# A new opening for an eight-core decoder kernel: order of the first loads, dummy matmuls, a shared first norm, and three conversions moved

## Chip, cores, metric

The kernel runs on all 8 cores of one Trainium2 chip, with the sequence split between the cores. The metric is the device time of the slowest core, in microseconds (us). Cores 0 to 3 are one die, 4 to 7 the other. In some executions one die or both run at a lower granted clock ("slow" state). Fast runs are compared with fast runs. A second measure is the **mean core span**: over all runs of a kernel, every die whose four cores all had a granted clock of 0.994 or more gives the mean of its four spans; the table gives the mean over such dies and its standard error. It is not the metric. The chips are called A to F, since kernels are only comparable on one chip: the same kernel before has a mean core span of 4998 us on some and 4994 us on others.

## The reference, cut

Two layers over x of shape (4, 8192, 1024), in float32:

```python
for l in range(DEPTH):
    x = x + 0.5 * swiglu(rms_norm(x, ffn1_norm[l]), ...)      # D_FF = 2816
    proj = rms_norm(x, mix_norm[l]) @ w_in[l]                   # q, k, v, u
    x = x + concat(rms_norm(window_attention), rms_norm(pooling)) @ w_out[l]
    x = x + cross_attention(rms_norm(x), rms_norm(mem), ...)
    x = x + 0.5 * swiglu(rms_norm(x, ffn2_norm[l]), ...)
return rms_norm(x, final_norm)
```

Only the first `rms_norm`, the first SwiGLU, and the loads of weights in the first 700 of 5000 us matter here.

## The kernel before

Each core works through nine tiles of up to 512 columns, twice (two layers). Matmuls are bf16, and weights arrive in 512 KB slots held in two rings: "F" (`sb_fr`, 6 slots, FFN weights) and "M" (`sb_mr`, 4 slots, all others). Weights lie in HBM as float32. A slot is either loaded and cast on the way by a DMA that GpSimd issues, or read as bf16 by a DMA that the sync engine (SP) issues. For the second kind a **conversion** must have run first: a DMA from HBM to HBM, issued by GpSimd, that waits for a certain matmul so that conversions spread over time. In the views below, `wf` and `wm` are the float32 weights of the two rings, `wfb` and `wmb` their bf16 copies, and `wab` is a bf16 tensor that the kernel itself has computed before and that SP loads into M slots. A load that casts on the way is called a cast load.

```python
def convert(kind, a, s):
    ...
    P._wait(P.E["pool"], [(id(pe.sem), pe.cnt - LAG)])
    P.dma("pool", rows(dst), rows(src), writes=(buf[a][s], cvb[i]), box=cvbox[i])
...
pre_conv = conv_list("wm", 0, 5, 9) + conv_list("wf", 1, 0, PRE)      # 34 conversions
...
elif v in (0, 1):
    ...
    run(sprinkle(fs, fill) if v else fs[:80] + sprinkle(fs[80:], pre_conv[:10]))   # fill = pre_conv[10:]
```

`fs` is the list of steps of a stage and `sprinkle` spreads conversions evenly over it. So 10 conversions stand in what is called the second stage here (v = 0), none in its first 80 steps, and 24 in the third (v = 1).

The opening:

```python
def x_chunks(ti, reads=()):                       # x of one tile, in four pieces of 512 KB
    for j in range(NPC):
        P.dma("act" if j % 2 else "sp", ...)      # two queues
        if ti == 0 and j == 0:
            P.dma("sp", vecs[:, :], vecs_d, writes=(constb,))

def first_norm(ti, dst, dstb):
    for c in range(NCH):                          # squares: odd chunks on VectorE, even on ScalarE
        ...
    ...                                           # 8 matmuls with ones sum over channels
    st.fin_act()                                  # Ln, Exp on ScalarE -> rst
    run(raw(h_steps(ti, 0, key, dst, dstb, 0, full=True)))   # 8 scales x * gain * rst on VectorE

# v == -1
P._wait(P.E["pool"], P._deps(xbs[0][:4], ())); advance("F", 0)    # slot 0 after half of tile 0's x
P._wait(P.E["pool"], P._deps(xbs[0], ()));     advance("F", 1)    # slot 1 after all of it
first_norm(0, hF, hFb)
x_chunks(1, (xbs[0][6], xbs[0][7]))
P._wait(P.E["pool"], P._deps(xbs[1], ()))                         # all of tile 1's x
advance("F", AHEAD["F"])                                          # slots 2 to 5
...
run(raw(g0[:5]))             # tile 0: gate and up of hidden chunks 0 and 1 (slots 0, 1)
first_norm(1, hM, hMb)
run(raw(g0[5:9] + g1[:9]))   # tile 0: chunk 2 (slot 2), then tile 1: chunks 0 to 2
```

The softmax here doesn't subtract the row's maximum and nothing guards it: scores larger than these inputs give would overflow.

## Time and profile before

| | us |
|---|---|
| median of 3 runs | 5008.35 (5007.73 to 5011.33) |
| core 0, the slowest in the profiled run | 5010.5 |
| the other seven cores | 4990.2 to 5000.8 |
| TensorE busy on core 0 | 4932.9 |

The first part of the profile's page gives busy time, share and number of instructions of each engine:

```profile
PE 4932.9 (98%) x25669; PEld 2437.3 (49%) x25669; DVE 2501.2 (50%) x4251; ACT 1666.9 (33%) x2862; POOL 983.1 (20%) x1058
```

TensorE is busy for 98%. Whatever the change wins must come out of the remaining 78 us, or out of matmuls that ran at half clock. The waits of TensorE on core 0 before 40 us (what ended the wait, us in total, how often, longest):

```profile
PE ps L351 <- DVE sb_kcarL L1198: 10.6, 1, 10.6
PE ps L351 <- DMA sb_fr<-wf: 3.5, 1, 3.5
PE ps L351 <- DVE sb_hF L488: 2.6, 1, 2.6
PE ps L351 <- DVE sb_pT L1209: 0.6, 1, 0.6
```

The first wait is for the matrix of ones, which VectorE fills only after the constants (`vecs`) have landed at 9.8 us, the third is Ln, Exp and the first scale, and the second is slot 2. The timeline of core 0 shows how these come about. Its columns are start, duration, engine, line, operation, output<-inputs, count, and in brackets the idle time before and what ended it:

```profile
8.60 1.15 ACT L149 ACTIVATE sb_pT<-sb_x 128x512 bf16<-128x512 f32 x2 [8.60 <-DMA sb_x<-xT]
9.81 0.43 DVE L1195 TENSOR_TENSOR sb_vecs<-sb_vecs 128x4 f32<-128x4 f32 x2 [9.81 <-DMA sb_vecs<-vecs]
12.25 1.15 ACT L149 ACTIVATE sb_pT<-sb_x 128x512 bf16<-128x512 f32 x2 [2.50 <-DMA sb_x<-xT]
16.66 5.39 DVE L488 SCALAR_TENSOR_TENSOR sb_hF<-sb_x,sb_vecs,sb_rst 128x512 bf16<-128x512 f32 x8 [3.10 <-ACT sb_esink L149]
17.56 12.48 PE L351 MATMUL ps<-sb_hF,sb_fr 128*128 128x512 bf16 x32 [2.63 <-DVE sb_hF L488]
...
28.14 2.11 POOL L159 DMA_DIRECT2D sb_fr<-wf  x4 [14.81 <-DMA sb_x<-xT]
35.21 3.61 PE L351 MATMUL ps<-sb_hF,sb_fr 128*128 128x512 bf16 x16 [3.46 <-DMA sb_fr<-wf]
38.66 10.52 PE L351 MATMUL ps<-sb_hM,sb_fr 128*128 128x512 bf16 x48
```

Half of tile 0's x is there at 8.6 us and the rest at 12.2. GpSimd waits until 28.1 us for tile 1's x before it asks for slot 2, and slot 2 ends TensorE's wait at 35.2 us. Tile 1's first gate matmul comes at 38.7. This last start is the marker for the opening below.

Much later, a second place that the change touches (timeline of core 0, same columns). A conversion goes out 0.57 us ahead of a cast load of an M slot, on the same queue, and TensorE then waits 4.6 us for that slot:

```profile
406.95 0.58 POOL L159 DMA_DIRECT2D wfb<-wf  x1
407.52 0.58 POOL L159 DMA_DIRECT2D sb_mr<-wm  x1
420.96 5.28 PE L351 MATMUL ps<-sb_hM,sb_mr 128*128 128x384 bf16 x16 [4.62 <-DMA sb_mr<-wm]
```

The 16 matmuls after the wait take 5.28 us; a warm group of 16 of this shape takes 2.76.

### The profile page before, as it was taken

The page shows a single profiled execution, that of the slowest core. Times are in us where ns is not written, and L with a number is a line of the kernel's source. Part 1 is how long each engine was busy: PE and PEld are TensorE (multiplying, and loading weights), DVE is VectorE, ACT ScalarE, POOL GpSimd, SP SyncE. Part 2 cuts the span into 40 slices and gives each one's busy share as a digit, 9 for nine tenths or more (in the row PEclk, how much of TensorE's full clock was granted, in tenths as well). Part 3 has the DMA queues.
Part 4 walks back from the last instruction along what each step waited for, and adds up shares of the span by engine and source line. Part 5 has one row for each costly group of instructions (what it writes and reads, how often), then busy time and mean ns, then how long its engine had stood idle before and what let it go on. Part 6 is the DMA issues. An engine that isn't in the chain of part 4 may idle for free.

```text
span 5010.5 us, 80089 instructions; the slowest of 8 cores (4990.2 to 5010.5 us)
## 1 busy us (share of the span) xinstructions
PE 4932.9 (98%) x25669; PEld 2437.3 (49%) x25669; DVE 2501.2 (50%) x4251; ACT 1666.9 (33%) x2862; POOL 983.1 (20%) x1058
## 2 busy tenths in 40 slices
PE   8999999999999999999999999999999999999998
PEld 3544454444454555554554544444444456455444
DVE  3245654454535363645454564635446454546452
ACT  3334432233332333332332333323323333333351
POOL 1222211212121121212120212211121212121111
PEclk9999999999999999999999999999999999999999
DMA  9998976677676887776786654444545556555434
GB/s 200 205 228 189 199 199 201 189 214 200 176 239 188 254 232 220 211 226 190 212 215 207 194 190 151 161 164 150 179 151 193 169 198 206 190 183 181 156 130 154
DMA packets 279558, 963.88 MB, mean 192 GB/s; under 512 B 30064, under 2 KB 31536, under 8 KB 278896
## 3 DMA queue, kind: packets, MB, share of 16 engines
q1 hardware_dynamic: 218016, 788.33, 48.3%
q0 software_dynamic: 60560, 168.32, 18.1%
q8 instruction: 221, 3.62, 0.3%
q10 hardware_dynamic: 576, 2.10, 0.1%
q14 instruction: 185, 1.52, 0.1%
HBM read 992.18 MB, written 130.02 MB: 224 GB/s over the span
## 4 chain that ended last, share of the span: by engine, by line
PE 91%; DMA 3%; DVE 2%; ACT 2%; issue 1%; POOL 0%; DVEq 0%; ACTq 0%; SPq 0%; POOLq 0%
PE ps L351 91%; DMA sb_fr<-wfb 1%; DMA sb_mr<-wm 1%; DMA sb_fr<-wf 1%; ACT sb_tmp L149 1%; ACT L146 1%; DVE sb_hM L488 0%; DVE sb_hF L488 0%; DMA sb_mr<-wab 0%; ACT sb_pT L149 0%; ACT sb_rst L149 0%; DVE sb_pT L843 0%; DVE sb_x L626 0%; DMA sb_x<-xT 0%; DVE sb_ao L891 0%
## 5 line engine op out<-in xcount | busy, mean ns | idle before, releaser
L351 PE MATMUL ps<-sb_hF,sb_fr 128*128 128x512 bf16 (+2 forms) x12320 | 2503.6, 360 | 25.0 <-DMA sb_fr<-wfb 8.8
L351 PEld LDWEIGHTS ps<-sb_hF,sb_fr 128*128 128x128 bf16 x12320 | 1201.7, 98 | 1234.5 <-issue 51.0
L351 PE MATMUL ps<-sb_act,sb_fr 128*128 128x512 bf16 (+2 forms) x6160 | 1263.2, 360 | 3.4 <-DMA sb_fr<-wf 2.7
L460 POOL TENSOR_TENSOR sb_acc<-sb_acc,sb_sqf 128x512 f32<-128x512 f32 (+3 forms) x522 | 627.9, 1203 | 2209.5 <-ACT sb_sqf L149 2142.7
L584 DVE TENSOR_TENSOR sb_act<-ps,sb_sg 128x512 bf16<-128x512 f32 (+2 forms) x770 | 489.7, 639 | 1061.4 <-PE ps L351 742.8
L351 PEld LDWEIGHTS ps<-sb_act,sb_fr 128*128 128x128 bf16 x6160 | 591.3, 98 | 616.3 <-issue 41.1
L149 ACT ACTIVATE sb_sg<-ps 128x512 f32<-128x512 f32 (+2 forms) x792 | 436.9, 557 | 1215.8 <-PE ps L351 941.5
L351 PE MATMUL ps<-sb_hM,sb_mr 128*128 128x512 bf16 (+2 forms) x3600 | 767.7, 359 | 6.3 <-DMA sb_mr<-wm 4.6
L149 ACT ACTIVATE sb_sqf<-sb_x 128x512 f32<-128x512 f32 (+2 forms) x553 | 324.0, 587 | 889.3 <-DVE sb_x L960 370.1
L351 PEld LDWEIGHTS ps<-sb_hM,sb_mr 128*128 128x128 bf16 x3600 | 352.0, 98 | 359.7 <-issue 13.9
L149 ACT ACTIVATE sb_pT<-ps 128x512 bf16<-128x512 f32 (+3 forms) x438 | 232.0, 561 | 375.0 <-PE ps L351 363.5
L626 DVE SCALAR_TENSOR_TENSOR sb_x<-ps,sb_x 128x512 f32<-128x512 f32 (+2 forms) x288 | 183.5, 637 | 259.3 <-PE ps L351 259.3
L720 DVE TENSOR_TENSOR sb_tmp<-ps,sb_sin 32x512 f32<-32x512 f32 (+2 forms) x360 | 229.1, 636 | 81.9 <-PE ps L351 52.1
L351 PE MATMUL ps<-sb_pT,sb_mr 128*128 128x512 bf16 (+4 forms) x1344 | 254.2, 345 | 9.6 <-DVE sb_pT L1120 3.7
L488 DVE SCALAR_TENSOR_TENSOR sb_hF<-sb_x,sb_vecs,sb_rst 128x512 bf16<-128x512 f32 (+2 forms) x280 | 218.0, 829 | 19.7 <-ACT sb_rst L149 16.6
L488 DVE SCALAR_TENSOR_TENSOR sb_hM<-sb_x,sb_vecs,sb_rst 128x512 bf16<-128x512 f32 (+2 forms) x296 | 191.5, 710 | 20.3 <-ACT sb_rst L149 20.3
L351 PEld LDWEIGHTS ps<-sb_pT,sb_mr 128*128 128x128 bf16 x1344 | 129.3, 98 | 130.1 <-issue 16.0
L960 DVE TENSOR_TENSOR sb_x<-ps,sb_x 128x512 f32<-128x512 f32 (+2 forms) x144 | 91.9, 639 | 185.1 <-PE ps L351 185.1
L1152 DVE TENSOR_TENSOR sb_x<-ps,sb_x 128x512 f32<-128x512 f32 (+2 forms) x144 | 92.1, 640 | 158.6 <-PE ps L351 158.6
L460 POOL TENSOR_TENSOR sb_ach<-sb_acc,sb_sqf 128x512 bf16<-128x512 f32 (+3 forms) x99 | 119.1, 1203 | 247.3 <-ACT sb_sqf L149 209.9
L149 ACT ACTIVATE sb_tmp<-sb_tmp 128x512 f32<-128x512 f32 (+3 forms) x204 | 124.5, 610 | 102.9 <-DVE sb_tmp L875 84.9
L146 ACT ACT_TABLE_LOAD x115 | 147.5, 1283 | 2.4 <-issue 0.3
(113 smaller groups left out, 2376.5 us busy)
## 6 DMA issues: line engine op xcount, KB each, us to landing
sb_fr<-wfb SPq DMA_DIRECT2D x1117, 512.0 KB, 4.7
sb_mr<-wmb SPq DMA_DIRECT2D x155, 512.0 KB, 4.6
sb_mr<-wab SPq DMA_DIRECT2D x144, 512.0 KB, 4.5
wfb<-wf POOLq DMA_DIRECT2D x96, 512.0 KB, 9.3
sb_fr<-wf POOLq DMA_DIRECT2D x38, 512.0 KB, 18.1
wfb<-sb_fr SPq DMA_DIRECT2D x36, 512.0 KB, 12.6
x<-sb_x POOLq DMA_DIRECT2D x20, 512.0 KB, 18.8
sb_x<-x POOLq DMA_DIRECT2D x20, 512.0 KB, 16.4
```

Of the source, the lines that this page charges most:

```text
L146: self.E["act"].h.preload_act_table_set(need)
L149: return self.op("act", lambda h: h.activation(out=out, in_=in_, func=func, scale=scale, **kw), reads, writes)
L351: P.op("pe", lambda h: h.matmul(out_ap, lt, rh, start=st, stop=sp_, skip_group_check=True), reads=list(rb), writes=(ob_,), signal=(i == n ...
L460: P.op("pool", lambda h: h.tensor_tensor(out=o[:, :T], in0=acc[a][:, :T], in1=sqf[s][:, :T], op=ALU.add), (accb[a], sqfb[s]), (ob_,))
L488: P.op("dve", lambda h: h.scalar_tensor_tensor(out=out_ap, in0=in_ap, scalar=vcol(col), in1=r[0], op0=ALU.mult, op1=ALU.mult), (in_b, r[1] ...
L584: P.op("dve", lambda h: h.tensor_tensor(out=a_, in0=d[1][0][:, :T], in1=sg[si][:, :T], op=ALU.mult), (d[1][1], sgb[si]), (ab_,))
L626: P.op("dve", lambda h: h.scalar_tensor_tensor(out=x_, in0=pp[:, :T], scalar=0.5, in1=x_, op0=ALU.mult, op1=ALU.add), (ppb, xb_), (xb_,))
L720: P.op("dve", lambda h: h.tensor_tensor(out=t1[lo:lo + 32, :W - c0], in0=pp[hi:hi + 32, :W - c0], in1=sinS[pr][lo:lo + 32, c0:W], op=ALU.m ...
L960: P.op("dve", lambda h: h.tensor_tensor(out=x_, in0=pp[:, :T], in1=x_, op=ALU.add), (ppb, xb_), (xb_,))
L1152: P.op("dve", lambda h: h.tensor_tensor(out=x_, in0=pp[:, :T], in1=x_, op=ALU.add), (ppb, xb_), (xb_,))
```

## The change

Intent: load tile 0's x in order on one queue, with the constants on the other; run 24 dummy matmuls meanwhile so that TensorE's clock is up; share the first norm's scales between VectorE and GpSimd; interleave gate and up of the first hidden chunk, so that both advance as scales come in; issue tile 1's x earlier, and let slots 2 to 5 wait for only half of it. Besides, 13 instead of 10 conversions go into the second stage.

```diff
 def x_chunks(ti, reads=()):
-        P.dma("act" if j % 2 else "sp", ...)
-        if ti == 0 and j == 0:
-            P.dma("sp", vecs[:, :], vecs_d, writes=(constb,))
+        P.dma("sp", ...)
...
+P.op("dve", lambda h: h.memset(actF[:, 0, :], 0.0), writes=(actb[0],))
 x_chunks(0)
-P.dma("sp", esink...); P.dma("sp", invc...)
+P.dma("act", vecs...); P.dma("act", esink...); P.dma("act", invc...)
+warm = ps_next()
+mms([(warm[0][:, :], warm[1], ones[:, :], actF[:, 0, :], (onesb, actb[0]), True, True) for _ in range(WARM)])   # 24
+ps_free(warm)
...
 def first_norm(ti, dst, dstb):
+    gc = (1, 4, 7)          # tile 0: x * gain of these chunks ahead of time on VectorE
...
     if ti == 0:
+        for c in (0, 2, 1, 3, 5, 4, 6, 7):
+            if c in gc: rstd_to(...)      # GpSimd: (x * gain) * rst
+            else:       scale_to(...)     # VectorE, as before
...
+                if pair and hc == 0:      # f_gu: gate and up of chunk 0 alternate, matmul by matmul
...
-first_norm(0, hF, hFb)
 x_chunks(1, (xbs[0][6], xbs[0][7]))
-P._wait(P.E["pool"], P._deps(xbs[1], ()))
+first_norm(0, hF, hFb)
+P._wait(P.E["pool"], P._deps(xbs[1][:4], ()))
...
-fill = pre_conv[10:]
+fill = pre_conv[13:]
-run(sprinkle(fs, fill) if v else fs[:80] + sprinkle(fs[80:], pre_conv[:10]))
+run(sprinkle(fs, fill) if v else fs[:80] + sprinkle(fs[80:], pre_conv[:13]))
```

More of the change, by code (lines that the diff above doesn't have):

```diff
@@ L40 @@
 NCV = 24
+WARM = 24
 PRE = 30
@@ L485, in done, with gain_to, rstd_to @@
                 give("rst", self.ri)
+        def gain_to(out_ap, out_b, in_ap, in_b, col):
+            P.op("dve", lambda h: h.tensor_scalar(out=out_ap, in0=in_ap, scalar1=vcol(col), scalar2=None, op0=ALU.mult), (in_b, constb), (out_b,))
+        def rstd_to(out_ap, out_b, in_ap, in_b, r):
+            P.op("pool", lambda h: h.tensor_tensor(out=out_ap, in0=in_ap, in1=r[0], op=ALU.mult), (in_b, r[1]), (out_b,))
         def scale_to(out_ap, out_b, in_ap, in_b, col, r):
@@ L558, in act_second, with f_gu @@
             return ubf[:, c:c + T], ub[g]
-        def f_gu(ti, l, f, src=None, act=act_main, shared=None):
+        def f_gu(ti, l, f, src=None, act=act_main, shared=None, pair=False):
             T = wide(ti, l) if f == 1 else tiles[ti][1]
@@ L587, in ev, with both @@
                     ps_free(d[1])
-                steps.append((lambda g=mmg: g(0), mmw(8, T)))
-                steps.append((lambda g=mmg: g(1), mmw(8, T)))
+                def both(hc=hc, d=d):
+                    slot, slb = d["slot"] = shared[hc] = load("F", "wf", l * 2 + f - 1, hc)
+                    d[0], d[1] = ps_next(), ps_next()
+                    mms([(d[part][0][:, :T], d[part][1], slot[:, (part * 8 + kc) * 128:(part * 8 + kc + 1) * 128], h_[:, kc, :T], (slb, hb_[kc]), kc == 0, kc == 7)
+                         for kc in range(8) for part in range(2)])
+                if pair and hc == 0:
+                    steps.append((both, mmw(16, T)))
+                    steps.append((lambda: None, 0.0))
+                else:
+                    steps.append((lambda g=mmg: g(0), mmw(8, T)))
+                    steps.append((lambda g=mmg: g(1), mmw(8, T)))
                 steps.append((ev, 0.0))
@@ L1185, in x_chunks @@
                 cs = slice(j * CPP, (j + 1) * CPP)
-                P.dma("act" if j % 2 else "sp", xw(ti, o + T)[:, cs, :], xblk(xT_d, OVER + c0 - o, o + T, j), reads=reads, writes=tuple(xbs[ti][cs]))
-                if ti == 0 and j == 0:
-                    P.dma("sp", vecs[:, :], vecs_d, writes=(constb,))
+                P.dma("sp", xw(ti, o + T)[:, cs, :], xblk(xT_d, OVER + c0 - o, o + T, j), reads=reads, writes=tuple(xbs[ti][cs]))
+        P.op("dve", lambda h: h.memset(ones[:, :], 1.0), writes=(onesb,))
+        P.op("dve", lambda h: h.memset(actF[:, 0, :], 0.0), writes=(actb[0],))
         x_chunks(0)
-        P.dma("sp", esink[:, :], sinkc_d, writes=(sinkb,))
-        P.dma("sp", invc[:, :], invc_d, writes=(invb,))
-        for l in range(L):
-            g0 = l * NVL + 44
-            P.op("dve", lambda h: h.tensor_tensor(out=vecs[:, g0:g0 + 4], in0=vecs[:, g0:g0 + 4], in1=vecs[:, g0 + 4:g0 + 8], op=ALU.mult), (constb,), (constb,))
-        P.op("dve", lambda h: h.memset(ones[:, :], 1.0), writes=(onesb,))
+        P.dma("act", vecs[:, :], vecs_d, writes=(constb,))
+        P.dma("act", esink[:, :], sinkc_d, writes=(sinkb,))
+        P.dma("act", invc[:, :], invc_d, writes=(invb,))
+        warm = ps_next()
+        mms([(warm[0][:, :], warm[1], ones[:, :], actF[:, 0, :], (onesb, actb[0]), True, True) for _ in range(WARM)])
+        ps_free(warm)
         for l in range(L):
@@ L1211, in first_norm @@
                     P.act(pT[:, c, :T], x_, AF.Square, (b_,), (pTb[c],))
+                if ti == 0 and c % 2:
+                    for g in gc:
+                        if g // 2 == c // 2:
+                            x_, b_ = xt(ti, 0, True)[g]
+                            gain_to(ao[:, gc.index(g), :T], aob[gc.index(g)][0], x_, b_, g)
             st.ps = ps_next()
@@ L1216, in first_norm @@
             if ti == 0:
-                P.act(esink[:, :], esink[:, :], AF.Exp, (sinkb,), (sinkb,))
-            run(raw(h_steps(ti, 0, key, dst, dstb, 0, full=True)))
+                for c in (0, 2, 1, 3, 5, 4, 6, 7):
+                    x_, b_ = xt(ti, 0, True)[c]
+                    if c in gc:
+                        rstd_to(dst[:, c, :T], dstb[c], ao[:, gc.index(c), :T], aob[gc.index(c)][0], st.r)
+                    else:
+                        scale_to(dst[:, c, :T], dstb[c], x_, b_, c, st.r)
+                st.done()
+                P.act(esink[:, :], esink[:, :], AF.Exp, (sinkb,), (sinkb,))
+                for l in range(L):
+                    g0 = l * NVL + 44
+                    P.op("dve", lambda h: h.tensor_tensor(out=vecs[:, g0:g0 + 4], in0=vecs[:, g0:g0 + 4], in1=vecs[:, g0 + 4:g0 + 8], op=ALU.mult), (constb,), (constb,))
+            else:
+                run(raw(h_steps(ti, 0, key, dst, dstb, 0, full=True)))
         def late_consts():
@@ L1322, in _build @@
                 advance("F", 1)
+                x_chunks(1, (xbs[0][6], xbs[0][7]))
                 first_norm(0, hF, hFb)
-                x_chunks(1, (xbs[0][6], xbs[0][7]))
-                P._wait(P.E["pool"], P._deps(xbs[1], ()))
+                P._wait(P.E["pool"], P._deps(xbs[1][:4], ()))
                 advance("F", AHEAD["F"])
@@ L1330, in _build @@
                 shared = {}
-                g0 = f_gu(0, 0, 1, shared=shared)
+                g0 = f_gu(0, 0, 1, shared=shared, pair=True)
                 g1 = f_gu(1, 0, 1, src=(hM, hMb), act=act_second, shared=shared)
```

## The prediction

> **Bound now.** The tensor engine: the page gives it 4932.9 of 5010.5 us busy (98%); the chain of waits is 91% matmul. Only part of core 0's 78 us of idle tensor time can be won, plus matmuls at half clock. By the tensor engine's waits, 17.3 us of it lies before 40 us: 10.6 us until the first ones-matmul, 2.6 us for Ln, Exp and first scale, 3.5 us for the third weight slot. Later ones the change can touch: 1.9 us at 106 us (wm slot), 4.6 us at 417 us (wm), 2.5 us (wab) and 1.8 us (wfb) at 630 to 690 us.
>
> **Opening before (timeline, core 0).** x's first half lands at 8.6 us, the rest at 12.2. VectorE waits for vecs to 9.8 us. First FFN matmul at 17.56; eight paced by 0.66 us scales, then half clock (0.43 us each) to about 27. Half of tile 1's x is issued by ScalarE at 16 us, behind Exp, and lands at 27.6; GpSimd then issues slots 2 to 5 at 28.1; DMA is empty from 26.3 to 29.7; slot 2 lands at 35.1, the dense stream starts at 35.2, tile 1's first gate matmul at 38.7.
>
> **The change.**
> 1. x in order on one queue, no vecs wait: the last piece lands at 11 to 12.5 us (slot 0's load starts earlier and competes), but one square per engine then remains: Exp about 1 us sooner.
> 2. GpSimd takes three scales (about 1.2 us each, from its other 128x512 operations), VectorE five: the first 16 matmuls end near 20 us, not 26.
> 3. 24 dummy matmuls, about 8 us in idle time. The Trainium skill ("TensorE: Matmul & The Clock Gate", Part 1) gives 3.4 us windows for warming and cooling; this trace roughly agrees (4.3 us of dense work before 0.43 became 0.22; after 3.2 us idle cores 1 and 3 were cold, core 0 after 3.5 us was not). Warmth may be lost again, and the next term binds anyway: about 0.
> 4. Tile 1's x all on the sync queue, not behind Exp: complete near 24 to 26 us. GpSimd waits for half of it: slots 2 to 4 issued near 20 us, slot 2 lands near 29 to 30. Main term. Tile 1's norm ends near 35 us, not 38.8. Together the dense stream shifts by 3.5 to 6 us; I take 4.5.
> 5. Three conversions move from the third stage (473 to 690 us) to the second (350 to 472). At 407 us a conversion went out 0.6 us ahead of the wm load on the same queue; with 13 spread evenly the nearest earlier one falls about 8 us sooner. The stall at 417 us (4.6 us on core 0, 0.9 to 2.8 on four others) and the half-clock matmuls after it (clock 0.72) mostly go: about -5 us on core 0, slowest by 10 us. Fewer later conversions: about -1.
> 6. Given back: DMA is saturated from 40 to 300 us, so slot waits near 106 and 200 us grow: +1.5.
>
> Sum: 5008.35 - 4.5 - 5 - 1 + 1.5 = about 4999.4 us, range 4991 to 5006. Faster by over 2%: 1%; within: 98%; slower: 1%.
>
> **Signs.** Right: slots 2 to 4 issued near 20 us; tile 1's first gate matmul near 33 to 35 us on core 0; no DMA gap at 26 to 30 us; the 417 us wait gone. Wrong: x landing after 13 us; a longer third-slot wait; new slot waits in 350 to 470 us.
>
> **What would make it wrong.** One queue moving x more slowly than two; GpSimd scales slowed beside VectorE; another core setting the time; conversions colliding with another load.

## The result

| | before | after |
|---|---|---|
| median, us | 5008.04 (4 runs, 5007.33 to 5011.33) | 5009.7 (4 runs, 5005.3 to 5013.83) |
| ratio of fast runs, 95% interval | | 1.0002 (0.9985 to 1.0019) |

The ratio is the mean time of one kernel's fast runs over that of the other's of the same rounds, so it is not quite the ratio of these medians. Nothing was gained: the forecast, 4999.4 of 5008.35 us, is a ratio of 0.9982 and lies just outside the interval.

The first line of the page (now of core 4, the slowest), then the core view of the profiled run after (span and granted clock), cut after core 5:

```profile
PE 4918.4 (98%) x25322; PEld 2440.5 (49%) x25693; DVE 2503.5 (50%) x4252; ACT 1666.3 (33%) x2862; POOL 987.9 (20%) x1061
```

```profile
core 0: 5001.1 us, clock 0.996
core 1: 4990.0 us, clock 0.997
core 2: 4989.4 us, clock 0.998
core 3: 4999.3 us, clock 0.997
core 4: 5012.3 us, clock 0.995
core 5: 5002.7 us, clock 0.996
```

The page's matmul counts cannot be set against each other, because some records are missing from the trace after. Core 0 went from 5010.5 to 5001.1 us, close to what was predicted for it, which was luck (see "The slowest core" below). Core 4 went from 5000.8 to 5012.3. Averaged over the eight cores of the two profiled runs the span is 4997.7 us before and 4998.9 after.

**The opening after.** TensorE's waits on core 0 before 40 us:

```profile
PE ps L352 <- DVE sb_hF L495: 4.3, 2, 3.7
PE ps L352 <- DMA sb_fr<-wf: 3.0, 2, 1.9
PE ps L352 <- ACT sb_pT L150: 2.4, 2, 1.4
PE ps L352 <- DVE sb_kcarL L1214: 2.0, 1, 2.0
```

The 10.6 us wait is gone from the list only because dummy matmuls fill it. The timeline of core 0 after:

```profile
13.18 0.63 ACT L150 ACTIVATE sb_pT<-sb_x 128x512 bf16<-128x512 f32 x1 [1.00 <-DMA sb_x<-xT]
16.64 6.52 DVE L495 SCALAR_TENSOR_TENSOR sb_hF<-sb_x,sb_vecs,sb_rst 128x512 bf16<-128x512 f32 x5 [2.35 <-ACT sb_esink L150]
16.68 4.60 POOL L492 TENSOR_TENSOR sb_hF<-sb_ao,sb_rst 128x512 bf16<-128x512 f32 x3 [2.28 <-ACT sb_esink L150]
18.64 2.72 PE L352 MATMUL ps<-sb_hF,sb_fr 128*128 128x512 bf16 x6 [3.67 <-DVE sb_hF L495]
24.43 2.18 POOL L160 DMA_DIRECT2D sb_fr<-wf  x4 [3.15 <-DMA sb_x<-xT]
26.50 3.61 PE L352 MATMUL ps<-sb_hF,sb_fr 128*128 128x512 bf16 x16 [1.11 <-DMA sb_fr<-wf]
33.70 3.61 PE L352 MATMUL ps<-sb_hF,sb_fr 128*128 128x512 bf16 x16 [1.87 <-DMA sb_fr<-wf]
37.15 1.67 PE L352 MATMUL ps<-sb_hM,sb_fr 128*128 128x512 bf16 x7
```

Slots 2 to 5 are asked for at 24.4 instead of 28.1 us. But on this core the last piece of x lands 0.9 us later (13.2), five scales on VectorE now take 6.52 us where eight took 5.39, and tile 1 starts at 37.2 us, 1.5 us sooner than before. Means over the eight cores, read from the same views:

| start, us | before | after |
|---|---|---|
| slot 0 asked for (half of tile 0's x landed) | 8.32 | 9.76 |
| slot 1 asked for (all of it landed) | 12.67 | 12.67 |
| first scale | 16.56 | 15.65 |
| first FFN matmul | 17.45 | 17.65 |
| slots 2 to 5 asked for | 28.00 | 23.60 |
| end of tile 1's last square on ScalarE | 28.18 | 27.94 |
| slot 2 first used | 34.45 | 32.96 |
| tile 1's first gate matmul | 38.91 | 37.73 |

So the opening gave 1.2 us at this marker in this pair of profiles. The eight cores of one profile differ there with a standard deviation of 2.3 us, so the size needs the repeats below.

**Where it went.** Each tile's mixer copies its last keys once, on GpSimd. These copies, "carry copies" in the expectations, cut the run into stages (timelines of core 0, before):

```profile
314.23 0.29 POOL L734 COPY sb_kcarL<-sb_kz 128x128 bf16<-128x128 bf16 x1 [17.81 <-DVE sb_kz L728]
492.05 0.29 POOL L734 COPY sb_kcarL<-sb_kz 128x128 bf16<-128x128 bf16 x1 [6.00 <-DVE sb_kz L728]
```

Means over eight cores of the start of the first copy, the time to the second ("second stage") and to the third ("third stage"), and the rest:

| us | first copy | second stage | third stage | rest |
|---|---|---|---|---|
| before | 310.8 | 172.4 | 192.8 | 4321.8 |
| after | 309.1 | 178.0 | 189.9 | 4321.9 |

The opening's 1.7 us and 3.0 us of the third stage are taken back by 5.7 us in the second. There the wait for `sb_mr<-wm` at 417 us is gone, as predicted, but on core 5, for instance, the waits of TensorE from 340 to 490 us begin with a load that never made it wait before:

```profile
PE ps L352 <- DMA sb_mr<-wab: 6.4, 2, 5.1
PE ps L352 <- ACT sb_sg L150: 1.3, 1, 1.3
```

and the timeline shows the two places, with half-clock matmuls after the longer one (4.96 us for 15, where a group of 16 takes 2.76):

```profile
435.25 1.46 PE L352 MATMUL ps<-sb_hM,sb_mr 128*128 128x384 bf16 x8 [1.35 <-DMA sb_mr<-wab]
...
455.33 4.96 PE L352 MATMUL ps<-sb_pT,sb_mr 128*128 128x384 bf16 x15 [5.09 <-DMA sb_mr<-wab]
```

These loads are asked for in good time. They are slow, though they go out on SP's queue and the conversions on GpSimd's. From issue to landing (min/median/max, view of the tensor `wab`, 395 to 470 us, core 5), first before, then after:

```profile
DMA to landing us min/median/max: 5.3/5.6/9.9
```

```profile
DMA to landing us min/median/max: 5.5/11.5/16.8
```

Core 5 has the largest difference in the median. Over the eight cores the medians are 5.6 to 9.2 us before and 9.2 to 12.0 after, and the longest of each core 8.1 to 11.9 before and 14.9 to 17.6 after.

TensorE's waits, mean over eight cores, summed from the same view on every core:

| us | 340 to 490 us: wm | wab | 490 to 690 us: wfb | wab |
|---|---|---|---|---|
| before (10 + 24 conversions) | 1.53 | 0.04 | 3.18 | 2.54 |
| after (13 + 21) | 0 | 5.35 | 0.20 | 2.44 |

This points at the three moved conversions. Rivals: chance in the slowest of eight cores, or the earlier opening, which makes TensorE meet the later loads sooner.

### The profile page after: what moved, and what is told of

Read it like the earlier page. It is cut to its first block, busy times and chain, and to the rows that moved or that the text cites. A ratio compares the mean times of both kernels' runs of the same rounds, so it can differ in the third digit from the quotient of the medians.

```text
span 5012.3 us, 79775 instructions; the slowest of 8 cores (4989.4 to 5012.3 us)
## 1 busy us (share of the span) xinstructions
PE 4918.4 (98%) x25322; PEld 2440.5 (49%) x25693; DVE 2503.5 (50%) x4252; ACT 1666.3 (33%) x2862; POOL 987.9 (20%) x1061
## 4 chain that ended last, share of the span: by engine, by line
PE 90%; DMA 4%; ACT 2%; DVE 2%; issue 2%; POOL 0%; DVEq 0%; ACTq 0%; SPq 0%; POOLq 0%
PE ps L352 90%; DMA sb_fr<-wfb 1%; DMA sb_mr<-wab 1%; ACT L147 1%; DMA sb_fr<-wf 1%; ACT sb_tmp L150 1%; DVE sb_hM L495 1%; DMA sb_x<-xT 0%; DVE sb_hF L495 0%; DMA sb_mr<-wm 0%; ACT sb_rst L150 0%; ACT sb_pT L150 0%; DVE sb_x L642 0%; DVE sb_pT L859 0%; ACT sb_sg L150 0%
## 5 line engine op out<-in xcount | busy, mean ns | idle before, releaser
L352 PE MATMUL ps<-sb_hM,sb_mr 128*128 128x512 bf16 (+2 forms) x3531 | 756.5, 358 | 9.3 <-DMA sb_mr<-wab 2.9
L352 PEld LDWEIGHTS ps<-sb_hM,sb_mr 128*128 128x128 bf16 x3600 | 351.3, 98 | 358.3 <-issue 11.9
L352 PEld LDWEIGHTS ps<-sb_pT,sb_mr 128*128 128x128 bf16 x1344 | 130.1, 99 | 136.8 <-issue 23.6
L160 POOL DMA_DIRECT2D wfb<-wf x96 | 55.4, 577 | 479.0 <-PE ps L352 478.1
## 6 DMA issues: line engine op xcount, KB each, us to landing
sb_fr<-wf POOLq DMA_DIRECT2D x38, 512.0 KB, 16.6
sb_x<-x POOLq DMA_DIRECT2D x20, 512.0 KB, 16.6
```

The source lines that it names most:

```text
L160: e.h.dma_start(out=out_ap, in_=in_ap).then_inc(box.sem, 16)
L352: P.op("pe", lambda h: h.matmul(out_ap, lt, rh, start=st, stop=sp_, skip_group_check=True), reads=list(rb), writes=(ob_,), signal=(i == n ...
```

## The experiments

In the expectations, which were written before each run, theory A is the explanation proposed at that time for what is tested (for conv13, that the moved conversions take back the gain), and the other theories are its rivals; each expectation says what they predict.

All kernels gave correct results. Each was run in five rounds beside the kernel before. "Before" in the tables is that of the same chip.

| chip | kernel | mean core span, us | dies counted | ratio of fast runs |
|---|---|---|---|---|
| A | after (the first comparison) | 4999.6 +- 0.9 | 8 | 1.0002 |
| B | before | 4993.7 +- 0.6 | 14 | |
| B | conv13 | 4995.5 +- 0.3 | 9 | 1.0005 (0.9982 to 1.0028) |
| B | open10 | 4993.4 +- 0.3 | 8 | 0.9998 (0.9969 to 1.0027) |
| B | open10_dve | 4993.3 +- 0.6 | 8 | 0.9999 (0.9970 to 1.0028) |
| B | open10_cold | 4992.4 +- 0.4 | 9 | none |
| C | before | 4997.5 +- 0.7 | 13 | |
| C | before2 | 4998.8 +- 0.6 | 10 | 0.9996 (0.9972 to 1.0020) |
| C | after2 | 5003.1 +- 0.8 | 6 | none |
| C | conv7 | 5007.2 +- 0.5 | 11 | 1.0018 (1.0000 to 1.0035) |
| C | open10_full | 4998.1 +- 0.6 | 13 | 0.9998 (0.9982 to 1.0013) |
| D | before | 4993.8 +- 0.5 | 8 | |
| D | half | 4991.3 +- 0.3 | 6 | none |
| D | conv10_dodge | 4997.0 +- 1.6 | 4 | none |
| D | conv13_early | 4989.1 +- 1.4 | 5 | none |
| D | half_early | 4989.0 +- 1.0 | 6 | none |
| E | before | 4998.2 +- 0.5 | 11 | |
| E | after3 | 5000.9 +- 0.9 | 13 | none |
| E | open10_b | 4999.0 +- 0.6 | 9 | none |
| E | half_b | 4998.7 +- 1.1 | 7 | none |
| E | half_early_b | 4991.6 +- 0.8 | 8 | none |
| F | before | 4994.1 +- 0.3 | 7 | |
| F | half_early_c | 4989.6 +- 0.4 | 5 | none |
| F | conv13_early_b | 4989.4 +- 0.4 | 7 | none |

"None": one of the two had too few fast runs.

The stages of the profiled runs, us, mean over the cores that were not throttled (all eight, or the four of one die):

| chip | kernel | cores | first copy | second stage | third stage |
|---|---|---|---|---|---|
| B | conv13 | 8 | 309.5 | 177.7 | 188.3 |
| B | open10 | 8 | 307.5 | 173.2 | 191.2 |
| B | open10_dve | 8 | 307.7 | 173.3 | 192.8 |
| B | open10_cold | 4 | 307.5 | 172.5 | 192.5 |
| C | before2 | 8 | 312.3 | 172.0 | 194.4 |
| C | conv7 | 8 | 310.9 | 170.4 | 204.4 |
| C | open10_full | 8 | 310.4 | 173.1 | 196.1 |
| D | conv10_dodge | 4 | 310.2 | 170.8 | 194.2 |
| D | conv13_early | 4 | 309.9 | 170.5 | 190.0 |
| D | half_early | 4 | 307.6 | 172.2 | 186.9 |
| E | after3 | 4 | 308.7 | 179.5 | 190.8 |
| E | open10_b | 8 | 311.6 | 173.6 | 193.7 |
| E | half_b | 8 | 311.2 | 172.7 | 193.6 |
| E | half_early_b | 4 | 309.9 | 172.9 | 190.6 |
| F | half_early_c | 4 | 308.2 | 171.4 | 188.5 |
| F | conv13_early_b | 4 | 309.6 | 171.2 | 187.6 |

The profiled runs of after2 and half were throttled on both dies and are left out.

### conv13: only the conversions moved

```diff
-fill = pre_conv[10:]
+fill = pre_conv[13:]
-... sprinkle(fs[80:], pre_conv[:10]))
+... sprinkle(fs[80:], pre_conv[:13]))
```

> The kernel before with one edit: 13 instead of 10 conversions in the second stage. Theory A (the moved conversions ate the opening's gain): the wait on the wm slot near 417 us goes, but waits on wab slots near 437 and 455 us of 2 to 5 us each appear on most cores with half-clock matmuls after them; the GpSimd carry copy near 485 us comes 4 to 7 us later after the one near 310 us than in before, and about 3 us of it come back by the copy near 677 us: ratio 1.0002 to 1.0010. Theory B (the prediction's term 5: the move helps): core 0's stall goes and nothing replaces it, ratio 0.9988 to 0.9995. Theory C (the order of conversions is neutral): ratio within 0.0002 of 1.

Measured: without any of the opening, the second stage takes 177.7 us and the third 188.3, as in after. TensorE's waits for wab from 340 to 490 us are 4.67 us in the mean over cores, for wm none. The mean core span is 1.8 us above before (standard error about 0.7). On core 1, for example, the waits of TensorE (340 to 490 us) begin with

```profile
PE ps L351 <- DMA sb_mr<-wab: 5.0, 1, 5.0
```

and the stretch from 400 to 450 us, in the view of windows (busy time and count of PE, PEld, DVE, ACT, POOL, then granted clock, DMA share, GB/s), reads, first before, then conv13:

```profile
400.00:450.00 50.00, 47.38 (x255) 24.53 (x254) 30.86 (x48) 17.50 (x34) 16.57 (x16) 1.00 0.84 200
```

```profile
400.00:450.00 50.00, 47.89 (x262) 25.29 (x263) 30.10 (x48) 17.91 (x36) 18.54 (x19) 1.00 0.98 203
```

The DMA engines go from 84% to 98% busy (from 83% to 99% in the mean over cores, while the bytes rise only from 191 to 204 GB/s). Theory A holds: the moved conversions bring the waits for wab. The ratio alone could not have shown it. Whether the full DMA engines alone explain the waits is looked at under conv13_early.

### open10: only the opening

```diff
-fill = pre_conv[13:]          # on the kernel after
+fill = pre_conv[10:]
-... pre_conv[:13]))
+... pre_conv[:10]))
```

> The kernel after with 10 conversions in the second stage: the opening alone. Theory A: the opening's gain of 1 to 2 us in the mean over cores stays, the wab waits near 437 and 455 us go, the wm wait near 417 us of 1 to 5 us returns: ratio 0.9992 to 0.9998. Theory B: without the conversions' move it is slower than the kernel after by about 5 us on the slowest core. Theory C: the opening itself gives its gain back later through slot waits before 300 us, then ratio 1.0000.

Measured: second stage 173.2 us, no wab wait, the wm wait back (1.66 us in the mean over cores). The first copy comes at 307.5 us, 2.0 us before that of conv13 on the same chip, which has the opening of before. The mean core span is 0.3 us under before, within its error, where theory A had expected 1 to 4 us.

### open10_dve: all eight first scales on VectorE

```diff
-gc = (1, 4, 7)     # on open10
+gc = ()
```

> open10 with all eight first scales on VectorE, none on GpSimd (and no gain products ahead). Theory A (GpSimd and VectorE slow each other: 1.75 us a scale beside GpSimd, 0.75 alone): scales take 0.75 us each again, the eight end within 5.4 us of Exp instead of 6.5, the first FFN matmul comes about 1.1 us sooner, the first group of 16 ends 1 to 2 us sooner; the total hardly moves (under 1 us), as slot 1 binds next. Rival: GpSimd's help is real and the slow scales have another cause: they stay above 1.2 us, and the first group ends later than in open10.

Measured, from the view of tile `sb_hF` on core 0 (count: duration ns min/median/max, first and last start), first open10, then open10_dve:

```profile
L495 DVE SCALAR_TENSOR_TENSOR sb_hF<-sb_x,sb_vecs,sb_rst x5: 739/1748/1851, 16.1 to 21.8; 128x512 bf16<-128x512 f32 x5
L492 POOL TENSOR_TENSOR sb_hF<-sb_ao,sb_rst x3: 1257/1705/1715, 16.1 to 19.0; 128x512 bf16<-128x512 f32 x3
```

```profile
L495 DVE SCALAR_TENSOR_TENSOR sb_hF<-sb_x,sb_vecs,sb_rst x8: 742/744/751, 15.0 to 19.6; 128x512 bf16<-128x512 f32 x8
```

Alone, a scale takes 0.74 us; beside GpSimd, 1.75. In the mean over cores the first FFN matmul comes at 16.71 instead of 17.89 us, and the first group of 16 ends 1.6 us sooner (ScalarE's first Silu at 22.60 instead of 24.20). The first copy does not move (307.7 against 307.5), so other things bind. Theory A is confirmed. The Trainium skill says it beforehand: "SBUF — State Buffer", "Who interferes with whom", has that a VectorE instruction with two SBUF inputs contends with a GpSimd instruction that reads SBUF; both are the case here.

### open10_cold: no dummy matmuls

```diff
-mms([(warm[0][:, :], warm[1], ones[:, :], actF[:, 0, :], ...) for _ in range(WARM)])   # on open10, with its memset
```

> open10 without the 24 dummy matmuls. Theory A (warmth is lost again or not binding): the first 16 matmuls run at half clock, 0.43 us each, but they are paced by the scales anyway; slot 1 and slot 2 still end the waits; tile 1's first gate matmul moves by under 1 us and the ratio to before equals that of open10 within 0.0003. Rival (warmth pays): tile 1's first gate matmul 3 to 4 us later than in open10.

Measured: tile 1's first gate matmul at 36.88 us in the mean over the undisturbed die, against 36.37 on the same die of open10; first copy at 307.5 on the undisturbed die; mean core span 1.0 us lower than open10. The dummies are worth nothing. In the kernel after, TensorE is cold again when it matters. The window from 15 to 20 us of core 0 (columns as above; the granted clock is third from the end), and the use of slot 2 on core 4 after 4 us of idling, where 16 matmuls take 6.48 us instead of 3.61:

```profile
15.00:20.00 5.00, 1.36 (x4) 0.43 (x4) 3.36 (x2) 2.81 (x5) 3.32 (x3) 0.50 0.93 227
```

```profile
33.57 6.48 PE L352 MATMUL ps<-sb_hF,sb_fr 128*128 128x512 bf16 x16 [3.97 <-DMA sb_fr<-wf]
```

### before2, after2: both kernels as they are, on chip C

No edit.

> The kernel before itself, for its trace on the same chip as the next ones and for the noise of the measure: ratio to before 1.0000 within 0.0004, mean core span equal within 1 us. Nothing is tested; theories agree.

> The kernel after itself on the same chip. Theory A (opening about -2 us by the first carry copy near 309 us, second stage +5, third stage -3): mean core span 0 to 2 us above before, ratio 1.0000 to 1.0006. Rival (the first comparison was chance and the prediction's sum of -9 us is right): ratio 0.998 to 0.999.

Measured: before2 lies 1.3 us above before with a standard error of about 0.9, which is the noise of the measure and was a little more than expected. after2 lies 5.6 us above before, more than either theory had. Only 6 dies of after2 were undisturbed.

### conv7: the dose the other way

```diff
-fill = pre_conv[10:]
+fill = pre_conv[7:]
-... pre_conv[:10]))
+... pre_conv[:7]))
```

> The kernel before with 7 instead of 10 conversions in the second stage, so 27 in the third: the dose the other way. Theory A (wab waits come from conversions close together in the second stage): second stage 2 to 4 us shorter than with 10 (no wm wait near 417 us, no wab wait), third stage 3 to 5 us longer; ratio 1.0000 to 1.0006. Rival (the number does not matter, only which load a conversion meets): both stages within 1.5 us of before.

Measured: the second stage is 1.6 us shorter than that of before2 (170.4 against 172.0), less than expected; the third is 10.0 us longer (204.4), far more. The mean core span is 9.7 us above before. On core 1 TensorE's waits from 490 to 690 us begin with

```profile
PE ps L351 <- DMA sb_mr<-wmb: 6.2, 1, 6.2
PE ps L351 <- DMA sb_fr<-wfb: 5.3, 1, 5.3
```

So both stages respond to the number of conversions, and steeply when it is too high: from 24 to 27 in the third stage costs 10.0 us, from 24 to 21 gains about 3. Theory A's direction is right, its sizes were not.

### open10_full: slots 2 to 5 wait for all of tile 1's x again

```diff
-P._wait(P.E["pool"], P._deps(xbs[1][:4], ()))    # on open10
+P._wait(P.E["pool"], P._deps(xbs[1], ()))
```

> open10, but GpSimd waits for all of tile 1's x before slots 2 to 5, as before the change. Theory A (the half-buffer wait only lets slots start about 3.5 us sooner, but slows the rest of x and slot 1): slots issued 3 to 4 us later than in open10, the third slot's wait longer by 1 to 3 us, tile 1's x complete up to 1 us sooner; tile 1's first gate matmul 0 to 2 us later than in open10, mean core span 0 to 2 us more. Rival (the half wait is worth the 4 us I predicted): tile 1's first gate matmul 4 us later.

Measured on chip C: slots asked for at 27.67 us (24.39 in after2), tile 1's first gate matmul at 39.61 (37.22 in after2, 40.86 in before2), the last square of tile 1 at 27.84 (28.15). Of the 3.6 us that after2 wins at this marker against before2, 2.4 would be the half-buffer wait, theory A's prediction but for 0.4 us more. This is weak evidence: after2's profile was throttled already in its first 40 us (granted clock 0.79 to 0.87 on core 0), and the cores of one profile differ by about 2 us here. The next experiments measure it better. The total cannot be compared with open10, which ran on another chip.

### half: only the half-buffer wait

```diff
-P.dma("act" if j % 2 else "sp", ...)               # x_chunks, on the kernel before
+P.dma("act" if j % 2 and ti == 0 else "sp", ...)
-first_norm(0, hF, hFb)
 x_chunks(1, (xbs[0][6], xbs[0][7]))
-P._wait(P.E["pool"], P._deps(xbs[1], ()))
+first_norm(0, hF, hFb)
+P._wait(P.E["pool"], P._deps(xbs[1][:4], ()))
```

> The kernel before with one part of the opening only: tile 1's x all on the sync queue, issued ahead of the first norm, and GpSimd waits for half of it before slots 2 to 5. No dummy matmuls, no GpSimd scales, tile 0's x on two queues, 10 conversions. Theory A (this part alone makes the opening's gain): slots 2 to 5 issued near 23.5 us in the mean over cores (28 before), third slot used near 32 to 33 us, first carry copy near 307.5 to 308.5 us as in open10, mean core span 1 to 3 us under before. Rival (the parts gain together): first carry copy within 1 us of before's 310 to 312 us.

Measured: slots asked for at 21.36 us, sooner than in any version with the whole opening (22.6 to 24.4); slot 2 first used at 31.47, tile 1's first gate matmul at 35.11. This profile was throttled on both dies; the fast one of half_b on chip E has 22.28, 32.07 and 35.52. The mean core span is 2.5 us under before. The first copy is read from half_early, which is the same up to there: 307.6 us, as in open10. Theory A.

### conv10_dodge: one conversion moved behind the wm load

```diff
-... fs[:80] + sprinkle(fs[80:], pre_conv[:10]))
+... place(fs, pre_conv[:10], [97, 114, 131, 147, 170, 181, 197, 214, 231, 247])   # 164 before; steps of fs
```

> The kernel before with one conversion of the second stage moved by six steps, from just ahead of the wm load near 407 us to just behind it; still 10. Theory A (the stall near 417 us is only that the load queues behind the conversion): the wm wait near 417 us goes on all cores, no wab wait over 2 us comes, second stage 170 to 172 us (172.0 to 173.3 with 10 so far), third unchanged; mean core span 0.5 to 3 us under before. Rival (any gain there returns as a wab wait): second stage 172 to 174 us and wab waits as in conv13.

Measured: no wm wait on any of the eight cores and a wab wait of 0.11 us in the mean (0.23 on the undisturbed die). The second stage takes 170.8 us, little more than the 170.4 of conv7. That part is clear: the stall at 417 us was only the load's place in the queue. The total is not: 3.2 us above before with an error of 1.7, from four dies. The stages do not explain it, and it stays open.

### conv13_early: 13 conversions, three of them where there were none

```diff
+... place(fs, pre_conv[:13], [39, 53, 66, 97, 114, 131, 147, 170, 181, 197, 214, 231, 247])
-fill = pre_conv[10:]
+fill = pre_conv[13:]
```

> As conv10_dodge, with the three extra conversions placed in the first third of the second stage (each just behind a wm load, before 350 us, where the kernel before has none), so 21 in the third. Theory A (13 hurt because they stand closer together while wab loads run, not because they are 13): second stage 171 to 174 us, third 188 to 190.5 as in conv13, mean core span 2 to 5 us under before, ratio 0.9990 to 0.9997. Rival (13 conversions do not fit in the second stage wherever they stand): second stage 176 us or more.

Measured: second stage 170.5 us, third 190.0, mean core span 4.7 us under before (error 1.5). TensorE waits neither for wm nor for wab from 340 to 490 us on any of the eight cores (the 2.7 us that remain in the mean are waits for other engines). The same 13 conversions that cost 5 us in the second stage cost nothing here when three of them stand in its first third. In the four later profiles of this placing, 0.6 to 2.6 us of DMA waits come back there (undisturbed die, against 4.7 to 6.2 in conv13, after and after3). Landing times of the wab loads on core 1, in before, conv13 and conv13_early:

```profile
DMA to landing us min/median/max: 5.3/6.4/8.1
```

```profile
DMA to landing us min/median/max: 5.1/10.6/16.6
```

```profile
DMA to landing us min/median/max: 5.2/9.8/11.5
```

The median has grown in both versions with 13; only conv13 has the load of 16.6 us, and only there TensorE waits for wab. Full DMA engines alone do not make TensorE wait either, as the windows of core 1 in conv13_early show: from 320 to 370 us, with the early conversions, they are as busy as in conv13 from 400 to 450 us, and TensorE does not stop.

```profile
320.00:370.00 50.00, 50.00 (x247) 23.24 (x246) 33.75 (x59) 19.40 (x32) 15.52 (x19) 1.00 1.01 214
400.00:450.00 50.00, 48.16 (x262) 25.24 (x261) 30.69 (x48) 18.14 (x36) 17.27 (x18) 1.00 0.90 201
```

So it is not the number in the stage but how many, or how close, run beside the wab loads: between the first and the last of these loads on core 1, five conversions go out in conv13, four in conv13_early and three in before. Number and closeness there were not separated.

### half_early: both together

> half and conv13_early together, to see whether the gains add: first carry copy as in half, second and third stage as in conv13_early; if theory A holds in both, mean core span 4 to 7 us under before, ratio 0.9985 to 0.9993, the fastest of all versions. Rival (slots or DMA time bind later): the sum of the parts less 2 us or more.

Edit: half and conv13_early. Measured: 4.8 us under before in mean core span, not the 7.2 that the two would add up to, although the profiled run shows both (307.6, 172.2, 186.9).

### after3, open10_b, half_b, half_early_b: four versions side by side on chip E

No new edits.

> The kernel after, once more, on the same chip as the next three. If opening (-2) and moved conversions (+2) simply add: mean core span within 1.5 us of before. If they interact (an earlier start meets the saturated DMA engines): 3 us or more above before, as the one earlier chip had it.

> open10 again (the opening alone). Against after3 it gives the conversions' cost within the change: theory A 1.5 to 4 us of mean core span under after3, nearly all in the second stage (173 against 178 us), with 2 to 3 us of it returned in the third. Against before: 0 to 2.5 us under.

> half again, on the same chip as open10: is the rest of the opening (tile 0's x on one queue, dummy matmuls, three engines for the first norm) worth anything? Theory A: no; first carry copy within 0.7 us of open10_b's, mean core span equal to open10_b's within 1.5 us. Rival 1 (the rest costs): half_b 2 us or more under open10_b. Rival 2 (the rest pays): 2 us or more above.

> half_early again, for a time in the fast state: mean core span 4 to 7 us under before, 2 to 5 under half_b (from the second and third stage), slowest core 4 to 8 us under before, ratio 0.9984 to 0.9993.

Measured: after3 is 2.7 us above before (error 1.0) and 1.9 above open10_b (error 1.1). Its second stage takes 179.5 us against 173.6, its third 190.8 against 193.7. So inside the change, too, the moved conversions take about 6 us and give back 3. half_b equals open10_b in the total (4998.7 and 4999.0) and in the first copy (311.2 and 311.6): the rest of the opening is worth nothing beside the half-buffer wait. At tile 1's first gate matmul it even costs: 37.45 us in open10_b, 35.52 in half_b. But on this chip neither beats before (4998.2). Here TensorE waits for DMA between 40 and 310 us for 2.6 us (open10_b) and 2.4 us (half_b) in the mean over cores, against 1.05 in before on chip A, 0.72 in before2 on chip C and 0.4 in open10 on chip B. Part of the earlier start may have returned as slot waits, as the prediction's term 6 had it. But after3 and half_early_b, which start as early on the same chip, wait only 0.95 and 1.2 us there (undisturbed die), and before was not profiled on it, so this is not shown. half_early_b is 6.6 us under before; its fast runs took 5000.03, 5005.19 and 5000.22 us, the single fast run of before 5005.12.

### half_early_c, conv13_early_b: what is the half-buffer wait worth at the end

No new edits.

> half_early a third time, for a ratio of fast runs, which the last two chips hardly gave for the kernel before: mean core span of undisturbed dies 4 to 7 us under before, ratio 0.9984 to 0.9993. Rival (its lead was chance): ratio 0.9996 or more.

> conv13_early again on the same chip: theory A 3 to 6 us under before in mean core span; half_early_c lies 0.5 to 3 us under it, the worth of the half-buffer wait after what slot waits before 310 us give back.

Measured on chip F: 4.5 and 4.7 us under before (errors 0.5). At the first copy half_early_c is 1.4 us ahead (308.2 against 309.6); at the end the two are equal. So the lead of the combined version is the placing of the conversions. A ratio of fast runs was not to be had on this chip.

## Why the prediction was wrong

It named 4999.4 us, range 4991 to 5006, and measured was 5009.7: no gain in place of 9 us.

**The step that failed is term 5**, the moved conversions: predicted -5 on core 0 and -1 later, measured about +2 in the mean core span (+1.8 in conv13, +1.9 between after3 and open10_b). Its first half was right: the 417 us stall goes (conv10_dodge shows that it was only queue order). But that stall was 4.6 us on core 0 and only 1.5 in the mean over cores. And the term left out what 13 conversions spread over the old stretch do to the other loads there. The DMA engines went from 83% to 99% busy from 400 to 450 us, the longest wab load of a core needed 14.9 to 17.6 us instead of 8.1 to 11.9, and TensorE waited 4.7 to 5.4 us for wab instead of 1.5 for wm. The prediction counted the load that a conversion no longer meets and not the loads that it meets now. It even listed "new slot waits in 350 to 470 us" as a sign of being wrong, and those came. The third stage gave 3 us instead of 1.

**Term 4 was right in mechanism, but little of it lasted.** Predicted -4.5 us; the whole opening gave 1.2 us at tile 1's first gate matmul (38.91 to 37.73) and 1.7 at the first copy on chip A, 2.0 at the first copy on chip B. The half-buffer wait alone came closer at that matmul: 34.42 us in half_early against 38.72 in conv13_early on chip D, 35.18 in half_early_c against 37.67 in conv13_early_b on chip F (undisturbed dies; these pairs differ in nothing else). Of these 4.3 and 2.5 us, 2.3 and 1.4 are left at the first copy and nothing at the end. They are means of four cores, which differ among themselves with a standard deviation of up to 4 us; where the gain goes is not shown. In the whole opening, slots were asked for 4.4 us sooner, but at 23.6 us, not near 20, and tile 1's x was complete no sooner (27.94 against 28.18), where 24 to 26 us was predicted. In the windows of 5 us from 5 to 25 us, core 0's DMA share was 0.92, 0.76, 0.93 and 0.97 in after, and 0.92, 0.88, 1.04 and 0.93 in before. That left another order little room to bring everything sooner. It was argued from these shares and not tested by itself.

**Term 2 was wrong.** Predicted: the first 16 matmuls end near 20 us. On core 0 they end at 25.4 (21.98 + 3.41 in the timeline). VectorE and GpSimd slow each other, 0.74 to 1.75 us a scale. It was named as a risk, and the rule stood in the skill's page (see open10_dve). It cost little, since open10_dve wins nothing at the first copy.

**Term 1 was right** for Exp (first scale 0.9 us sooner), not for x: the last piece was to land at 11 to 12.5 us and came at 12.67 in the mean, no sooner than before, and at 13.2 on core 0, past the prediction's own sign of being wrong (13 us). The first half came 1.4 us later than before, which was not foreseen.

**Term 3 was right**: the dummies are worth nothing, and the clock was lost again. The Trainium skill's "TensorE: Matmul & The Clock Gate", Part 1, gives cooling after an idle window of about 3.4 us. Here 16 matmuls were warm after 1.9 us of idling (3.61 us for 16) and cold after 4.0 us (6.48 us). In between it is no sharp edge: in before, core 3 took 5.30 us for 16 after 3.14 us, and core 0 took 3.61 after 3.46.

**Term 6 is open.** DMA waits of 2.4 to 2.6 us before 310 us came in two profiles on chip E, not in the others with the early start (1.2 us at most on undisturbed dies), and conv13_early_b, with the old opening, had 1.2 as well. What becomes of the opening's last 1 to 2 us where those waits are small is not settled: open10 on chip B is 2.0 us ahead at the first copy and 0.3 (error 0.7) at the end.

**The slowest core.** The prediction treated core 0's 10 us as a fault of core 0 that could be mended. Core 0 did come down to 5001 us, and core 4 took its place at 5012. In 106 pairs of undisturbed runs of the kernel before (cores 0 and 1, 2 and 3, and so on) the first core of the pair was the longer in 54, and the two differed by 9.4 us in the median. Which core of a pair is slower looks like chance, so what helps one core alone can hardly be counted on in the metric. The Trainium skill's "HBM Reference", "Specifications (TRN2)", says that the two cores of a pair share the bandwidth of one HBM domain. That fits; no run here changed it on purpose.

conv13_early and half_early beat both kernels in mean core span: 4.5 to 6.6 us (0.09 to 0.13%) under before on three chips (conv13_early on two of them). In the metric, the slowest core, a gain is not shown: there were too few fast runs for a ratio.

## What to carry to other kernels

When background transfers are moved, look not only at the load that they stop delaying but at the loads that run in the stretch they move to, and at how long each may take before an engine waits for it. The same 13 conversions cost 5 us in a stage when all stood in its last two thirds and next to nothing when three stood in the first. The busy share alone does not tell: at about 100% TensorE waited for 5 us in the one stretch and for nothing in the other. A gain of a few microseconds at the start has to be followed stage by stage, on all cores, because little of it may be left at the end: 2.5 to 4.3 us at the first tiles were nothing after 5000. And do not plan on the slowest core of one profile when cores swap that place from run to run.

## What the Trainium skill lacked or had wrong

- "SBUF — State Buffer", "Who interferes with whom": has the rule for two SBUF inputs but no size for this pair of instructions. Here a VectorE scale of 128x512 with two SBUF tensors went from 0.74 to 1.75 us beside a GpSimd product of two SBUF tensors, which went from 1.26 (shortest) to 1.71 us. Five scales and three products took 6.52 us together; eight scales alone took 5.39.
- "HBM Reference": gives the shared bandwidth of a pair, but not that one core of each pair falls behind, by 9.4 us of 5000 in the median of 106 pairs, and that it is either one. That the shared bandwidth is the reason was not tested.
- "TensorE: Matmul & The Clock Gate", Part 1: nothing wrong was found. The profile's granted clock should be read with care: in before it says 1.00 for 20 to 25 us on core 0, where the matmuls from 22.6 us on followed one another every 0.43 us.
- "DMA: Bandwidth & Descriptors": no rate for a load that casts float32 to bf16 on the way. Here such loads alone, with the DMA engines 99% busy, moved 134 GB/s (30 to 35 us, core 0, before), against 263 GB/s from 15 to 20 us with x and one such load together. The profile counts 512 KB for such a load, the size of the bf16 slot, and the float32 weights that it reads are twice that: by reading, 134 would be 268 GB/s (an estimate), so the figures do not show that casting is slow.
